# Transposes of the probabilities two bursts behind their scores, values one burst later, in a hybrid decoder trunk

## The chip, the cores and the metric

The kernel runs on one core of a Trainium2 chip. The metric is device time in microseconds (us) of one execution, the median of several runs.

## What is computed

The reference is a two-layer decoder trunk for one sequence of 1024 positions and width 1024, in fp32. Layer 0 feeds one projection into a dilated attention with 16 heads of 64 and a pooling branch, each gated, and projects back; layer 1 does the same with a spatial gating unit and an S5 state-space layer. After each comes a cross-attention into 256 memory tokens. The change touches the dilated attention alone:

```python
sc = jnp.einsum('nbihd,nbjhd->nbhij', qb, kb, preferred_element_type=jnp.float32)
sc = jnp.where(valid[None, :, None], sc, NEG)
m = jnp.max(sc, axis=-1, keepdims=True)
p = jnp.exp(sc - m)
den = jnp.sum(p, axis=-1, keepdims=True)
o = jnp.einsum('nbhij,nbjhd->nbihd', (p / den).astype(v.dtype), vb)
...
a_out = dilated_attention(q, k, v).reshape(b, s, A_WIDTH) * jax.nn.silu(g_a)
```

The three patterns (windows 128, 512, 2048 with dilations 1, 4, 16) are mixed by their softmax denominators.

## The kernel before

Large products are made of three matmuls each (high x high, high x low, low x high part of an fp32 number), with a moving tile of 128x512; a projection half (one 512-wide half of the sequence for one block of 128 channels) is 8 such triples, 24 matmuls, `mm3` at lines 206 to 208, or lines 472 to 474 for the values' own projection. Weights come by SP's queue, ScalarE makes the high part (line 180), VectorE the low part (line 181).

In the first layer's stage two generators run interleaved. `ab_main` is the projections, gates and the pooling branch. `ab_side` is the attention: 8 pairs of heads with 8 blocks of 128 queries each, so 64 bursts, numbered `n`; a burst does both heads of a pair (called halves here). `drive` takes one step of the side for about every two steps of the main, so TensorE's order has in most gaps between bursts 24 projection matmuls, in about one of six 12. The order of TensorE within the stage is then pinned as recorded (`in_order`); on the other engines a scheduler decides it.

A burst's work is in four functions made by `attn`:

- `front(b)`: the scores, 32 small matmuls into two PSUM buffers `ps_s` (line 536); VectorE adds the mask into an SBUF tile `P` and so reads the buffers (line 543), joins the two dilated parts (546), takes the maximum (547); ScalarE exponentiates (548), VectorE inverts the sum (549), ScalarE scales (550).
- `turn(b)`: per half, TensorE transposes `P` into a PSUM buffer `ps_t` (lines 567 and 570); VectorE copies the near part to `PT` (576), ScalarE the far part to `PTr` (580), which GpSimd has zeroed (563).
- `mix(b)`, every second burst: the values for two bursts, `PT` against `V`, into `ps_o` (line 593).
- `last(half)`, every fourth burst: the far values (line 605), then VectorE multiplies by the gate (609) and `put_g` stores the result from GpSimd's queue (621).

The tags `ps_mm`, `ps_s`, `ps_t` and `ps_o` have two PSUM buffers each. `P`, `PT`, the gated results and other half-size tiles share 14 SBUF buffers. GpSimd meanwhile prepares tables for the S5 layer (`s5_prep`, started from `behind`); it uses two of the same PSUM tags, with transposes at line 1154, copied by ScalarE at line 1155.

In the loop of `ab_side` before, step `n` issues the transposes of burst `n - 1`, then the scores of burst `n`, and on odd steps the values of bursts `n - 3` and `n - 2`.

Of the kernel before, what the change touches and what calls it, by code (L numbers as in the profile page):

```python
# [98 lines left out]
class Prog:  # L99
# [524 lines left out]
    def ab_side(s):  # L624


        prep, made = s.s5_prep(), {}
        for n in range(64 + 2):
            pr, b = divmod(n, 8)
            if n < 64:  # L630
                while pr not in s.pair or (b == 3 and pr not in s.gated):
                    yield 0
                if b == 0:
                    made[pr] = s.attn(pr)
            if 0 < n <= 64:
                was, wb = divmod(n - 1, 8)
                made[was][1](wb)
            if n < 64:
                made[pr][0](b)
            if n > 2 and n % 2 == 1:  # L640
                was, wb = divmod(n - 3, 8)
                made[was][2](wb)
                if n % 4 == 1:
                    made[was][3](wb // 4)
            yield 1
            if n > 6 and n < 64:
                s.behind(prep)
        while s.behind(prep) is not None:
            yield 1
# [912 lines left out]
```

## Time and profile before

| | us |
|---|---|
| median of 3 runs | 2097.26 |
| lowest, highest | 2096.18, 2103.48 |
| the profiled execution | 2095.89 |
| its span, first to last instruction | 2094.0 |

The profile is of one execution. Busy times are per engine; PE is TensorE's matmuls, PEld its weight loads, DVE is VectorE, ACT ScalarE, POOL GpSimd, and DVEq is VectorE's sequencer. Matmuls overlap in the pipeline, so the distance of their starts is the measure of their pace, not their length. An idle time in brackets stands before the instruction, with what ended it.

### The profile page before, as it was taken

To read this page: it belongs to the slowest core of one execution; us is meant where nothing else is said; L and a number is where in the kernel's file an instruction comes from. 1 tells how busy PE (TensorE), PEld (TensorE's weight loads), DVE (VectorE), ACT (ScalarE), POOL (GpSimd) and SP (SyncE) were. 2 spreads that over 40 slices of the span, in tenths; PEclk is the share of its full clock that TensorE was granted. 3 is DMA by queue.
4 is the path that set the end of the run, shared out by engine and by line. 5 is a ranking of instruction groups with operands and counts; after the bars stand their busy time and mean duration, and the time that the engine had idled before them with its cause. 6 is when DMAs were issued, how large, how long until landed. Compare 5 with 4: busy or idle time off the path is not lost. (4 is left out here: it accounts for less than half of the span.)

```text
span 2094.0 us, 31894 instructions
## 1 busy us (share of the span) xinstructions
PE 2035.1 (97%) x12350; PEld 1686.6 (81%) x12350; DVE 1094.8 (52%) x1987; ACT 803.3 (38%) x1618; POOL 532.7 (25%) x802
## 2 busy tenths in 40 slices
PE   8999999999999988999999999999999999999998
PEld 8998877777776766888888888888888887888887
DVE  6665055645456565456444555444653335554544
ACT  7766134355334443114333443212221123434443
POOL 5332006822334255221111003221221100210013
PEclk9999999999999989999999999999999999999999
DMA  8888202113122122116444035522431125641142
GB/s 300 302 284 293 86 30 64 62 56 117 53 78 74 56 77 86 69 73 240 163 165 166 31 126 181 175 91 71 137 98 68 66 95 172 206 156 70 56 166 81
DMA packets 129159, 258.68 MB, mean 124 GB/s; under 512 B 12784, under 2 KB 58992, under 8 KB 129008
## 3 DMA queue, kind: packets, MB, share of 16 engines
q1 hardware_dynamic: 86608, 189.52, 26.7%
q0 software_dynamic: 13440, 43.53, 5.6%
q10 hardware_dynamic: 28960, 23.60, 3.6%
q8 instruction: 97, 1.59, 0.3%
q14 instruction: 54, 0.44, 0.1%
HBM read 193.16 MB, written 63.44 MB: 123 GB/s over the span
## 5 line engine op out<-in xcount | busy, mean ns | idle before, releaser
L181 DVE TENSOR_TENSOR wl<-wst,wh 128x1024 fp32r<-128x1024 f32 (+1 forms) x263 | 348.6, 1339 | 112.7 <-ACT wh L180 108.3
L206 PE MATMUL ps_mm<-xg,wh 128*128 128x512 f32 x928 | 371.8, 401 | 1.9 <-DVE ug L1367 1.5
L207 PE MATMUL ps_mm<-xg,wh 128*128 128x512 f32 x928 | 364.7, 393 | 0.0
L208 PE MATMUL ps_mm<-xg,wl 128*128 128x512 f32 x928 | 364.2, 392 | 0.0
L180 ACT ACTIVATE wh<-wst 128x1024 fp32r<-128x1024 f32 (+1 forms) x263 | 262.6, 1016 | 103.0 <-PE ps_mm L207 82.7
L206 PEld LDWEIGHTS ps_mm<-xg,wh 128*128 128x128 f32 x928 | 175.7, 189 | 47.8 <-issue 8.5
L208 PEld LDWEIGHTS ps_mm<-xg,wl 128*128 128x128 f32 x928 | 175.7, 189 | 37.1
L207 PEld LDWEIGHTS ps_mm<-xg,wh 128*128 128x128 f32 x928 | 175.9, 190 | 34.6 <-issue 0.2
L243 POOL TENSOR_TENSOR acc<-acc,sq 128x512 f32<-128x512 f32 (+1 forms) x81 | 103.6, 1279 | 212.5 <-ACT sq L239 206.2
L226 ACT ACTIVATE xg<-x,gains 128x512 fp32r<-128x512 f32 x64 | 46.2, 722 | 240.0 <-DVE x L782 182.9
L548 ACT ACTIVATE P<-P,mx 128x192 f32<-128x192 f32 (+7 forms) x128 | 65.8, 515 | 137.4 <-DVE mx L547 136.1
L580 ACT ACTIVATE PTr<-ps_t 128x128 f32<-128x128 f32 (+2 forms) x192 | 43.1, 271 | 159.2 <-DVE PT L576 154.8
L576 DVE TENSOR_TENSOR PT<-ps_t,cst 128x256 f32<-128x256 f32 (+1 forms) x128 | 47.0, 402 | 61.5 <-PE ps_t L570 61.1
L543 DVE TENSOR_TENSOR P<-ps_s,cst 128x320 f32<-128x320 f32 (+7 forms) x128 | 65.3, 551 | 19.0 <-PE ps_s L536 17.6
L227 DVE SCALAR_TENSOR_TENSOR xg<-x,gains,xg 128x512 fp32r<-128x512 f32 x64 | 52.4, 819 | 43.1 <-ACT xg L226 43.1
L621 POOL DMA_DIRECT2D gab<-G x32 | 18.4, 574 | 207.9 <-DVE G L609 83.6
L1367 DVE TENSOR_TENSOR ug<-ps_mm,R 128x512 f32<-128x512 f32 x32 | 22.1, 689 | 90.4 <-PE ps_mm L208 90.3
L567 PE MATMUL ps_t<-cst,P 128*128 128x128 f32 x128 | 36.0, 293 | 33.6 <-ACT P L550 30.8
L207 PE MATMUL ps_s<-gr,wh 128*128 128x512 f32 x168 | 65.6, 390 | 2.0 <-DVE gr L214 2.0
L206 PE MATMUL ps_s<-gr,wh 128*128 128x512 f32 x168 | 65.5, 390 | 1.2 <-ACT gr L213 1.2
L208 PE MATMUL ps_s<-gr,wl 128*128 128x512 f32 x168 | 65.4, 389 | 0.0
L550 ACT ACTIVATE P<-P,den 128x192 f32<-128x192 f32 (+7 forms) x128 | 60.3, 510 | 10.0 <-DVE den L549 10.0
(424 smaller groups left out, 4878.0 us busy)
## 6 DMA issues: line engine op xcount, KB each, us to landing
wst<-w_ab SPq DMA_DIRECT2D x40, 512.0 KB, 3.3
wst<-w_out_ab SPq DMA_DIRECT2D x32, 512.0 KB, 3.8
wst<-vsc SPq DMA_DIRECT2D x32, 512.0 KB, 4.0
wst<-w_kv SPq DMA_DIRECT2D x31, 512.0 KB, 6.3
wst<-w_cd SPq DMA_DIRECT2D x24, 512.0 KB, 3.7
wst<-w_out_cd SPq DMA_DIRECT2D x32, 384.0 KB, 3.6
wst<-w_q SPq DMA_DIRECT2D x16, 512.0 KB, 8.3
msc<-mo ACTq DMA_DIRECT2D x32, 256.0 KB, 6.3
```

Of the source, the lines that this page charges most:

```text
L180: s.last_hi = s.nc.scalar.activation(H[:, :w], t[:, :w], AF.Copy)
L181: s.nc.vector.tensor_tensor(L[:, :w], t[:, :w], H[:, :w], op=ALU.subtract)
L206: s.nc.tensor.matmul(ps, lhsT=lh, rhs=rh, start=(i == 0), stop=False)
L207: s.nc.tensor.matmul(ps, lhsT=lh, rhs=rl, start=False, stop=False)
L208: s.nc.tensor.matmul(ps, lhsT=ll, rhs=rh, start=False, stop=(i == n - 1))
L226: nc.scalar.activation(H, x, AF.Copy, scale=g)
L227: nc.vector.scalar_tensor_tensor(L, x, g, H, op0=ALU.mult, op1=ALU.subtract)
L243: nc.gpsimd.tensor_tensor(st["acc"][:, :n], st["acc"][:, :n], q[:, :n], op=ALU.add)
L543: nc.vector.tensor_tensor(t[:, :n], p[e][:, :n], s.cst[:, m0:m0 + n], op=ALU.add)
L548: j = nc.scalar.activation(t[:, :m], t[:, :m], AF.Exp, bias=mx, accum_out=den)
L550: k = nc.scalar.activation(t[:, :m], t[:, :m], AF.Copy, scale=den)
L576: nc.vector.tensor_tensor(PT[b // 2, e][:, c0 + 128 * j0:c0 + 256].rearrange("p (j i) -> p j i", i=128), src, s.cst[:, C_NM + 128 * j0:C_N ...
```

## The change

The side's loop issues the transposes of burst `n - 2` at step `n` instead of `n - 1`. The values follow on even steps instead of odd ones, one step later, and the loop is one step longer.

```diff
-        for n in range(64 + 2):
+        for n in range(64 + 3):
...
-            if 0 < n <= 64:
-                was, wb = divmod(n - 1, 8)
+            if 1 < n <= 65:
+                was, wb = divmod(n - 2, 8)
                 made[was][1](wb)
             if n < 64:
                 made[pr][0](b)
-            if n > 2 and n % 2 == 1:
-                was, wb = divmod(n - 3, 8)
+            if n > 3 and n % 2 == 0:
+                was, wb = divmod(n - 4, 8)
                 made[was][2](wb)
-                if n % 4 == 1:
+                if n % 4 == 2:
                     made[was][3](wb // 4)
```

TensorE's order at the start of attention, where the second burst's scores stand (a piece of the difference; `ps_t<-cst,P` is a transpose of probabilities, `ps_s<-kk,q` scores, `ps_mm` a projection):

```order
 L207 MATMUL ps_mm<-xg_1548,wh 128x512
 L208 MATMUL ps_mm<-xg_1548,wl 128x512
-L567 MATMUL ps_t<-cst,P 128x128
-L570 MATMUL ps_t<-cst,P 128x128
-L567 MATMUL ps_t<-cst,P 128x128
-L570 MATMUL ps_t<-cst,P 128x128
 L536 MATMUL ps_s<-kk,q 32x256 x8
 L536 MATMUL ps_s<-kk,q 32x64 x8
```

The first burst's transposes have left the place ahead of the second burst's scores; they stand ahead of the third burst's now, and each later burst's likewise.

VectorE's order around the sixteenth burst's first pass (line 543, width 512), with buffer numbers; `PT<-ps_t` copies a transpose. Before:

```order
330 L543 TENSOR_TENSOR P_4354<-ps_s_4336,cst_84 128x512
331 L543 TENSOR_TENSOR P_4363<-ps_s_4337,cst_84 128x512
332 L181 TENSOR_TENSOR wl_4463<-wst_4292,wh_4462 128x1024
333 L546 TENSOR_TENSOR P_4354<-P_4354 128x128
334 L546 TENSOR_TENSOR P_4363<-P_4363 128x128
335 L547 TENSOR_REDUCE mx_4355<-P_4354 128x1
336 L547 TENSOR_REDUCE mx_4364<-P_4363 128x1
337 L549 RECIPROCAL den_4356<-den_4356 128x1
338 L549 RECIPROCAL den_4365<-den_4365 128x1
339 L576 TENSOR_TENSOR PT_4324<-ps_t_4401,cst_84 128x256
```

And now:

```order
328 L543 TENSOR_TENSOR P_4338<-ps_s_4320,cst_84 128x512
329 L543 TENSOR_TENSOR P_4347<-ps_s_4321,cst_84 128x512
330 L181 TENSOR_TENSOR wl_4449<-wst_4278,wh_4448 128x1024
331 L546 TENSOR_TENSOR P_4338<-P_4338 128x128
332 L546 TENSOR_TENSOR P_4347<-P_4347 128x128
333 L547 TENSOR_REDUCE mx_4339<-P_4338 128x1
334 L576 TENSOR_TENSOR PT_4382<-ps_t_4378,cst_84 128x256
335 L576 TENSOR_TENSOR PT_4390<-ps_t_4386,cst_84 128x256
336 L547 TENSOR_REDUCE mx_4348<-P_4347 128x1
337 L549 RECIPROCAL den_4340<-den_4340 128x1
338 L543 TENSOR_TENSOR P_4412<-ps_s_4394,cst_84 128x160
```

The copies of the previous burst's transposes now stand between the two halves' maxima (line 547); before, both maxima and both reciprocals came ahead of the next copies.

TensorE's order after the last scores of the attention; `ps_o<-PT,V` are values. Before:

```order
L536 MATMUL ps_s<-kk,q 32x256 x16
L593 MATMUL ps_o<-PT,V 64x128 x2
L593 MATMUL ps_o<-PT,V 64x256 x2
L593 MATMUL ps_o<-PT,V 64x128 x2
L206 MATMUL ps_mm<-plr,wh 128x512
L207 MATMUL ps_mm<-plr,wh 128x512
```

And now:

```order
L208 MATMUL ps_mm<-plr,wl 128x512
L567 MATMUL ps_t<-cst,P 128x128
L570 MATMUL ps_t<-cst,P 128x128 x2
L567 MATMUL ps_t<-cst,P 128x128
L570 MATMUL ps_t<-cst,P 128x128 x2
L593 MATMUL ps_o<-PT,V 64x128 x2
L593 MATMUL ps_o<-PT,V 64x256 x2
L593 MATMUL ps_o<-PT,V 64x128 x2
```

The values that stood right behind the last scores now stand behind the transposes that follow six projection matmuls later.

## Rows read from the trace of the kernel before

**Rows 1.** The page's first part: busy us, share of the span, instructions.

```profile
PE 2035.1 (97%) x12350; PEld 1686.6 (81%) x12350; DVE 1094.8 (52%) x1987; ACT 803.3 (38%) x1618; POOL 532.7 (25%) x802
```

**Rows 2.** Stretches: length, then PE, PEld, DVE, ACT, POOL busy; clock, DMA share, GB/s.

```profile
270.00:825.00 555.00, 520.57 (x4680) 401.86 (x4679) 318.44 (x771) 242.56 (x655) 232.22 (x477) 0.96 0.21 68
...
570.00:590.00 20.00, 15.54 (x125) 11.16 (x131) 11.79 (x27) 8.62 (x23) 1.15 (x2) 0.83 0.30 91
...
740.00:750.00 10.00, 8.91 (x66) 7.09 (x66) 3.36 (x13) 3.61 (x12) 10.00 (x36) 0.83 0.01 2
760.00:780.00 20.00, 13.06 (x109) 9.20 (x110) 14.39 (x28) 9.71 (x27) 9.32 (x15) 0.74 0.41 146
800.00:820.00 20.00, 14.75 (x92) 10.01 (x90) 9.15 (x21) 7.09 (x21) 12.32 (x17) 0.83 0.33 119
```

**Rows 3.** Waits of TensorE, 270 to 825 us: total us, times, longest.

```profile
PE ps_t L567 <- ACT P L550: 30.8, 15, 4.1
PE ps_t L567 <- ACT s5wz L1155: 2.7, 1, 2.7
```

**Rows 4.** Timeline of TensorE, a quiet burst: start, us, instruction.

```profile
443.66 1.04 PE L536 MATMUL ps_s<-kk,q 64*32 64x256 f32 x32
...
450.22 0.27 PE L567 MATMUL ps_t<-cst,P 128*128 128x128 f32 x1
```

**Rows 5.** Timeline of TensorE, scores and transposes at waits, idle in brackets.

```profile
424.26 0.93 PE L536 MATMUL ps_s<-kk,q 64*32 64x256 f32 x32
...
431.91 0.47 PE L567 MATMUL ps_t<-cst,P 128*128 128x128 f32 x1 [3.79 <-ACT P L550]
...
433.06 0.47 PE L567 MATMUL ps_t<-cst,P 128*128 128x128 f32 x1 [0.24 <-ACT P L550]
...
575.88 0.48 PE L567 MATMUL ps_t<-cst,P 128*128 128x128 f32 x1 [2.66 <-ACT P L550]
...
577.74 0.48 PE L567 MATMUL ps_t<-cst,P 128*128 128x128 f32 x1 [0.95 <-ACT P L550]
...
750.18 0.77 PE L536 MATMUL ps_s<-kk,q 64*32 64x256 f32 x32
...
762.88 0.45 PE L567 MATMUL ps_t<-cst,P 128*128 128x128 f32 x1 [3.50 <-ACT P L550]
...
767.60 0.48 PE L567 MATMUL ps_t<-cst,P 128*128 128x128 f32 x1 [4.06 <-ACT P L550]
...
804.97 0.48 PE L567 MATMUL ps_t<-cst,P 128*128 128x128 f32 x1 [3.69 <-ACT P L550]
```

**Rows 6.** Timeline of TensorE, projection matmuls after the wait at 767.

```profile
771.02 0.63 PE L206 MATMUL ps_mm<-xg,wh 128*128 128x512 f32 x1
...
772.30 0.63 PE L206 MATMUL ps_mm<-xg,wh 128*128 128x512 f32 x1
```

**Rows 7.** Timelines of VectorE and GpSimd, 750 to 768 us.

```profile
750.86 6.31 DVE L708 TENSOR_TENSOR win<-vb 128x1023 f32<-128x1023 f32 x1
...
762.08 4.91 DVE L181 TENSOR_TENSOR wl<-wst,wh 128x512 fp32r<-128x512 f32 x1 [1.17 <-ACT wh L180]
...
754.04 2.04 POOL L938 TENSOR_TENSOR s5w<-Ei,trig 128x512 f32<-128x512 f32 x2
...
765.18 1.25 POOL L938 TENSOR_TENSOR Ei<-s5w,s5w 128x512 f32<-128x512 f32 x1
```

**Rows 8.** Timelines of TensorE, VectorE, ScalarE: one burst's scores to its probabilities.

```profile
475.45 0.83 PE L536 MATMUL ps_s<-kk,q 64*32 64x256 f32 x32
...
476.37 0.96 DVE L543 TENSOR_TENSOR P<-ps_s,cst 128x352 f32<-128x352 f32 x2 [0.27 <-PE ps_s L536]
...
479.00 0.84 ACT L550 ACTIVATE P<-P,den 128x224 f32<-128x224 f32 x2
```

**Rows 9.** Line 543: waits in VectorE's queue, ns min/median/max.

```profile
L543 DVEq EVENT_SEMAPHORE  x35: 21/21/1022, 271.5 to 783.4; - x35
```

**Rows 10.** DMA issues of the gates' stores: count, KB each, us to landing.

```profile
gab<-G POOLq DMA_DIRECT2D x32, 256.0 KB, 2.5
```

## The prediction

> **What bounds the kernel now.** I read the busy shares first: TensorE is busy 97% of the span, VectorE 52%, ScalarE 38%, GpSimd 25% [rows 1]. So only what TensorE waits for, or does slowly, can be won. The table of stretches puts the loss in one place: the attention stage, 270 to 825 us, is the long stretch with a lowered granted clock, 0.96, and 34 us without a matmul (555.0 less 520.6) [rows 2]. The list of who waited for whom, for TensorE in that stretch, names it: 30.8 us in 15 waits of the probabilities' first transpose (line 567) for ScalarE's last pass over the same probabilities (line 550), then 2.7 us in one wait of that transpose for the S5 preparation's copy (line 1155), and next to nothing else [rows 3].
>
> The timeline of TensorE shows the pattern. In a quiet burst the scores (line 536) end at 444.70 and the transposes of that burst start at 450.22, with 24 projection matmuls between: 5.5 us, 0.23 us each, and no wait [rows 4]. The probabilities are ready some 3.6 us after the scores (scores end 476.28, line 550 ends 479.84) when VectorE and ScalarE are free [rows 8], so 5.5 us suffices. About every sixth gap holds 12 matmuls, 2.8 us, and in some places the two engines are late as well; there TensorE stands. Five waits make 17.7 of the 30.8 us [rows 5]. After most of them the projection matmuls start 0.427 us apart instead of 0.23 (three in 1.28 us) [rows 6], and the 10 or 20 us around show a granted clock of 0.74 to 0.83 [rows 2]: a wait is paid twice, once standing and once at the 1.2 GHz level of the two.
>
> **The change part by part.** No instruction is added or removed. *Transposes two bursts behind.* The first burst's transposes now follow the scores of two further bursts, as the first piece of TensorE's order shows; from then on each burst's transposes are separated from its scores by one more gap, one more set of scores and transposes. That adds at least 2.8 + 0.4 + 0.5 = 3.7 us, mostly 6.5. At 424 to 432 us the scores ended at 425.19 and the transposes began at 431.91, 6.7 us later [rows 5]. The new distance there is 2.8 us (12 matmuls), the next transposes and scores of about 1.6, and 24 matmuls of 5.5, so 9.9 us: covered. The same sum covers the waits at 575.88 (a 12-matmul gap too) and 804.97, the latter with little to spare. So I take the 30.8 us as removed, before what is given back.
>
> *The clock.* The deficits are 4 x 1.7 (10 us at 0.83, of which the row from 740 stands for four, the others from 300, 430 and 670), 3.4 (570 to 590), 5.2 (760 to 780) and 3.4 (800 to 820), 18.8 us [rows 2]. A stretch at half clock costs half its length, which is this deficit, only where TensorE was working. In three of the windows it stood for 4.06, 0.95 and 0.24 us between slow transposes [rows 5], which takes half of those off, 2.6 us. So 16.2 us go with the waits, if all go. Together 47.0 us.
>
> *What stays.* At 750.95 the scores end, and the two halves of their probabilities come at 762.9 and 767.6 [rows 5]. The new distance is 24 matmuls 5.5, transposes and scores 1.4, values and far values 2.9, 12 matmuls 2.8: 12.6 us, so 763.5. The first half is in time, the second 4 us late. Its cause is no queue distance: a VectorE add took 6.31 us and a split of weights 4.91 us, and each ended about a microsecond after a row of GpSimd's work did (757.2 after 756.1, 767.0 after 766.4) [rows 7]; that work is not touched. I leave the 4.06 us and the slow stretch behind it (twice 5.2 us at half clock, less the standing, halved: 3.2 us) in the sum: 7.3 us. The S5 wait of 2.7 us is not the change's and stays.
>
> *Values one burst later.* They moved with the transposes: in the order's last piece the values follow the transposes of a later burst, and between a transpose and the values that use it lies one gap, as before. VectorE's copy and ScalarE's copies have that gap still. At the end of attention the last far values come after 24 more projection matmuls; more of these follow, so nothing stands. The gates' stores on GpSimd's queue follow a step later, and are read only in the output projection. Cost nought; with the cover gone it would be one gap, 5.5 us, once.
>
> *New waits.* The transposes had held the next scores back until the previous probabilities were done. Now the scores wait only for VectorE to have read their two PSUM buffers (line 543). It does so 1.05 us after the scores when free [rows 8] against a gap of at least 2.8, so nought is the lower end; where a VectorE instruction is held up as at 750 us it is up to 6.3 less 2.8, 3.5 us in a place [rows 7]. Nearer the first: 2 us in all, an estimate.
>
> Sum: 30.8 + 16.2 - 7.3 - 2 = 37.7 us. The profiled execution took 2095.9 us (span 2094.0), 1.4 under the median of the runs shown; from its own time, 2058 us.
>
> **The rivals.** *The other engines become the late ones.* VectorE's new order at the second place shows the second half's maximum of a burst standing behind the copies of the previous burst's transposes, which TensorE issues only before the next scores; so probabilities come later there by most of a gap, and part of the new distance is spent. If this and the GpSimd collisions keep the three worst places (4.06 + 3.50, 3.69, 2.66 + 0.95 us standing; 3.2 + 3.4 + 2.9 slow), 24.4 us stay and the gain is 22.6: 2073 us. For it: these three have VectorE or ScalarE late, not only a short gap. Against: in the order the displaced maxima still come a gap ahead of their own transposes. The Trainium skill ("SBUF — State Buffer", the section on the two separate sides) says that VectorE and GpSimd share a port pair under an exclusive lock, so the loser stands for the whole of the other's instruction. The 6.31 us add agrees in kind, and spans several GpSimd rows in sequence [rows 7]; by this rule collisions move but do not vanish.
>
> *The buffers run out, and it is slower.* A probability tile lives a burst longer, so two more of the 14 half-size buffers are taken, and VectorE's first pass (line 543) may stand until a gate's store on GpSimd's queue has freed one. Up to a delay of about 5.5 - 1.05 = 4.5 us the gap hides it; beyond that the scores stand. GpSimd works through the preparation for 10 us and more without a break (10.00 of 10 from 740) [rows 2], and a gate's store lands 2.5 us after its issue [rows 10]: 10 + 2.5 - 4.5 = 8 us lost per case, so from six such cases on (48 against 47 us) the change is slower; at twelve, of the 16 gates stored in the stage, 2096 - 47 + 96 = 2145 us. Against: before, VectorE's queue stood at most 1.02 us for anything ahead of that pass [rows 9], and as many of these instructions wait for such a store in the new order (17) as in the old. The Trainium skill ("Perfetto Trace Analysis", Optimization Strategy) reads a gap that repeats on the saturated engine as a possible lack of SBUF or PSUM for the next tile. By that the waits would not be cured by distance and could grow. Here the waits name line 550's data, not a buffer [rows 3].
>
> *The waits change their name only.* If VectorE and ScalarE could not keep up on average, TensorE would stand at the scores for the same sum: 2096 us. They are busy 57% and 44% of the stage (318.4 and 242.6 of 555.0) [rows 2], so this is unlikely.
>
> **How the numbers follow.** The forecast, 2058 us, has 0.60, the late engines 0.27, the renamed wait 0.08, the buffers 0.05. The lower end of the range is all 47.0 us and the S5 wait of 2.7 with 1.7 of slow clock, 51.4: 2044 us. The upper takes in the late engines with room for half as much again of what stays, 24.4 x 1.4 = 34, a gain of 13: 2083 us. Outside lie the last two cases and a tail of the second. Half a percent, 10.5 us, is about what a measurement of this kernel can tell from no change. Faster by more: all of the first and nearly all of the second, 0.86; within: 0.09; slower: 0.05.
>
> **What would show it.** Right, if the list of TensorE's waits between 270 and 825 us has under 8 us left for line 567 behind line 550, the granted clock of the stage is 0.98 or more, and the stage ends 35 to 40 us earlier while the rest of the span keeps its length. The wait that stays would stand where the pooling's first adds meet GpSimd's rows. The second case shows as waits of line 567 that remain at three or four places, with VectorE rows of 2 to 6 us ahead of them. The third shows as waits of line 536 behind line 543 and of VectorE behind GpSimd or a store. The forecast is wrong if the waits go and the time doesn't, which would mean that a later stage waits for something that attention used to be slower than.

## The result and the profile after

The changed kernel takes 2059.99 us (2057.86 to 2062.47, four runs), against 2098.97 us (2096.18 to 2103.48) of the kernel before: ratio 0.9823, 95% interval 0.9807 to 0.984. The forecast was 2058, the range 2044 to 2083. The profiled executions have spans of 2094.0 and 2057.4 us, so 36.6 us are to be accounted for. One of the four executions of the run called e4 below took 7101 us and is left out; its time is the median of the other three.

The page of the kernel after: busy us, share of the span and instructions.

```profile
PE 2020.7 (98%) x12350; PEld 1680.1 (82%) x12350; DVE 1102.9 (54%) x1987; ACT 800.2 (39%) x1618; POOL 539.9 (26%) x802
```

The same instructions run [rows 1]; TensorE's busy time is 14.4 us shorter with as many matmuls, the first sign of a faster clock. The stretches of the kernel after, attention's stage and two lowered pieces of it: length, then PE, PEld, DVE, ACT, POOL busy; clock, DMA share, GB/s.

```profile
270.00:785.00 515.00, 503.09 (x4632) 392.26 (x4631) 325.55 (x768) 238.38 (x651) 234.63 (x472) 0.99 0.22 70
...
490.00:500.00 10.00, 7.39 (x76) 5.75 (x77) 5.73 (x14) 5.24 (x16) 0.61 (x1) 0.83 0.28 83
690.00:700.00 10.00, 9.12 (x70) 6.72 (x69) 7.43 (x22) 4.00 (x10) 4.34 (x5) 0.83 0.03 8
```

TensorE stands 11.9 us in the stage (515.0 less 503.1) instead of 34.4 [rows 2], and those two are the only 10 us pieces with a lowered clock; in all others of the stage it is 1.00. What TensorE still waits for, from the list of who waited for whom in the stage of the kernel after (us in total, times, longest):

```profile
PE ps_t L567 <- ACT s5wz L1155: 5.1, 2, 3.5
PE ps_t L1154 <- ACT PTr L580: 2.6, 2, 2.4
PE ps_t L567 <- ACT PTr L580: 1.8, 3, 1.2
PE ps_mm L206 <- DVE G L738: 1.4, 1, 1.4
PE ps_s L536 <- DVE ktr L1165: 0.9, 1, 0.9
```

The line that led this list before, line 567 behind line 550 [rows 3], is gone. All five rows are new or longer, and three of them are about the two buffers `ps_t`, not about the probabilities (the row of `s5wz` had 2.7 us [rows 3], that of line 1154 0.8).

The gain is kept to the end. Line 842 is a matmul of the cross-attention behind the first layer; its group, with the first and last start, in the kernel before:

```profile
L842 PE MATMUL ps_o<-wh,xg x96: 387/389/481, 1140.8 to 1989.2; 128*128 128x512 f32 x96
```

and in the kernel after:

```profile
L842 PE MATMUL ps_o<-wh,xg x96: 387/389/481, 1105.6 to 1952.9; 128*128 128x512 f32 x96
```

Its first one starts 35.2 us earlier and its last 36.3 us, so the rest of the program keeps its length to about a microsecond.

### The profile page after: what moved, and what is told of

It reads as the page before. It is cut to its first block, busy times and chain, and to the rows that moved or that the text cites. A ratio compares the mean times of both kernels' runs of the same rounds, so it can differ in the third digit from the quotient of the medians.

```text
span 2057.4 us, 31828 instructions
## 1 busy us (share of the span) xinstructions
PE 2020.7 (98%) x12350; PEld 1680.1 (82%) x12350; DVE 1102.9 (54%) x1987; ACT 800.2 (39%) x1618; POOL 539.9 (26%) x802
## 4 chain that ended last, share of the span: by engine, by line
PE 86%; DVE 5%; ACT 2%; issue 1%; DMA 1%; POOL 1%; DVEq 0%; ACTq 0%; POOLq 0%
PE ps_mm L206 13%; PE ps_mm L207 13%; PE ps_mm L208 13%; PE ps_s L207 4%; PE ps_s L208 4%; PE ps_s L206 4%; PE ps_o L208 3%; PE ps_o L207 3%; PE ps_o L206 3%; PE ps_s L536 2%; PE ps_mm L1340 1%; PE ps_mm L1338 1%; PE ps_mm L1339 1%; PE ps_o L593 1%; PE ps_mm L472 1%
## 5 line engine op out<-in xcount | busy, mean ns | idle before, releaser
L208 PEld LDWEIGHTS ps_mm<-xg,wl 128*128 128x128 f32 x928 | 174.3, 188 | 36.9
L1367 DVE TENSOR_TENSOR ug<-ps_mm,R 128x512 f32<-128x512 f32 x32 | 22.1, 689 | 90.4 <-PE ps_mm L208 90.3
L239 ACT ACTIVATE sq<-x 128x512 f32<-128x512 f32 (+1 forms) x77 | 44.8, 582 | 42.6 <-DVE x L890 37.9
L536 PE MATMUL ps_s<-kk,q 64*32 64x256 f32 (+7 forms) x2048 | 58.4, 332 | 0.9 <-DVE ktr L1165 0.9
```

The source lines that it names most:

```text
L208: s.nc.tensor.matmul(ps, lhsT=ll, rhs=rh, start=False, stop=(i == n - 1))
L536: i = nc.tensor.matmul(p[e][32 * r:32 * r + 32, c], lhsT=q[rows[e], 128 * b + 32 * r:128 * b + 32 * r + 32], rhs=x, start=True, stop=True)
```

## A ledger of the runs

Two sums tell nearly every span below. *Standing* is TensorE's idle time from 270 to 830 us. *Slow* is the sum, over the 56 pieces of 10 us there, of 10 us times one less the granted clock. Where a piece was both idle and slow a little is counted twice (2.6 us before).

| kernel | standing | slow | sum | span |
|---|---|---|---|---|
| before | 34.4 | 20.4 | 54.8 | 2094.0 |
| e1, even gaps, one behind | 29.1 | 10.2 | 39.3 | 2078.8 |
| e12, values later alone | 45.0 | 25.3 | 70.3 | 2107.2 |
| e2, values left on odd steps | 22.1 | 13.7 | 35.8 | 2075.8 |
| e3, change in the second half | 19.4 | 8.5 | 27.9 | 2071.9 |
| after | 11.9 | 3.4 | 15.3 | 2057.4 |
| e4, S5 transposes in the projections' PSUM | 8.5 | 3.4 | 11.9 | 2055.3 |
| e6, 16 half-size and 41 large buffers | 8.8 | 3.4 | 12.2 | 2057.5 |
| e5, three behind, buffers of e6 | 16.6 | 5.1 | 21.7 | 2070.0 |
| e7, 13 half-size buffers | 26.5 | 11.9 | 38.4 | 2084.4 |
| e9, two half-size buffers freed | 6.4 | 0.0 | 6.4 | 2047.9 |
| e11, e9 with even gaps | 10.5 | 5.1 | 15.6 | 2057.5 |
| e10, before, with the buffers of e9 | 39.8 | 22.1 | 61.9 | 2099.2 |

Span less sum lies between 2037 and 2048 us throughout, though the spans differ by 59. One run is not in the table: e8, without the S5 preparation in the stage, loses its time behind 830 us. Between before and after, 22.5 us of standing and 17.0 of slow clock make 39.5; less the 2.6 that were counted twice, 36.9 of the 36.6 us.

## Is it the short gaps, or the distance?

The theory was that a burst's probabilities come too late over a gap of 12 matmuls, so that a distance of two bursts, or simply no short gap, would cure it. The first run keeps the order of before and makes all gaps but two 24 matmuls long.

```diff
-        drive(tc, s.ab_main(), s.ab_side(), 0.55, -500)
+        drive(tc, s.ab_main(), s.ab_side(), 0.5, -500)
```

> The kernel before, transposes one burst behind, but with a side rate of 0.5 instead of 0.55, so that all gaps between bursts but two near the end hold 24 projection matmuls. Theory (the waits came from gaps of 12 matmuls that are shorter than the probabilities' latency): the waits at gaps of 12 were 2.20 + 2.03 + 4.03 + 0.30 + 3.61 + 2.03 + 3.69 + 1.56 = 19.5 us of the 30.8, with 11 us of slow clock behind them; most of that goes, so 25 to 30 us faster than before, about 2070, and 10 us behind the change. Rival (VectorE and ScalarE are late whatever the gap): under 10 us faster, 2090.

Measured: 2080.8 us, ratio 0.993 (0.9903 to 0.9956). TensorE's waits in the stage of this kernel:

```profile
PE ps_t L567 <- ACT P L550: 28.7, 13, 9.0
PE ps_t L567 <- ACT s5wz L1155: 0.4, 1, 0.4
```

The two waits of the last burst, from its timeline of TensorE:

```profile
812.27 0.47 PE L567 MATMUL ps_t<-cst,P 128*128 128x128 f32 x1 [8.96 <-ACT P L550]
...
815.82 0.48 PE L567 MATMUL ps_t<-cst,P 128*128 128x128 f32 x1 [2.64 <-ACT P L550]
```

The standing behind line 550 hardly shrank, 28.7 us against 30.8 [rows 3]; the slow clock halved. Of the 28.7 us, 11.6 are these two, where in this order the pooling's add stands beside GpSimd's preparation and takes 3.73 us (at 796.26). The rest is spread: nine of the eleven longest waits are between 0.95 and 2.64 us. The gain of 15.7 us lies between what the theory and the rival gave. So the short gaps were under half of the story: one burst behind, even 24 matmuls are too short wherever VectorE or ScalarE is late. The distance itself was needed.

The next run makes the change from burst 32 on only.

```diff
-            if 1 < n <= 65:
-                was, wb = divmod(n - 2, 8)
-                made[was][1](wb)
+            for t in (n - 1, n - 2):
+                if 0 <= t < 64 and t + (1 if t < 32 else 2) == n:
+                    made[t // 8][1](t % 8)
...
-            if n > 3 and n % 2 == 0:
-                was, wb = divmod(n - 4, 8)
-                made[was][2](wb)
-                if n % 4 == 2:
-                    made[was][3](wb // 4)
+            for t in (n - 3, n - 4):
+                if 0 <= t < 64 and t % 2 == 0 and t + (3 if t < 32 else 4) == n:
+                    made[t // 8][2](t % 8)
+                    if t % 4 == 2:
+                        made[t // 8][3](t % 8 // 4)
```

> The change for bursts 32 to 63 only; bursts 0 to 31 keep their transposes one behind. Theory (each wait is local, so gains add up by place): the waits of bursts 0 to 31, 9.9 us in the trace of before, and the slow clock behind two of them, 3.3 us, come back: 13 us more than the change, 2073. Rival (what counts is the later part, where VectorE meets GpSimd's preparation): 2062.

Measured: 2073.2 us, ratio 0.9888 (0.9862 to 0.9915). The first row of its waits:

```profile
PE ps_t L567 <- ACT P L550: 9.7, 7, 3.8
```

The waits are local: behind line 550, those of the half that keeps the old distance stay, the others go, and the time follows.

## Do the values have to move along?

The prediction put the values' move at no cost and took it as part of the whole. Two runs part them. First the change with the values left on odd steps:

```diff
-        for n in range(64 + 3):
+        for n in range(64 + 2):
...
-            if n > 3 and n % 2 == 0:
-                was, wb = divmod(n - 4, 8)
+            if n > 2 and n % 2 == 1:
+                was, wb = divmod(n - 3, 8)
...
-                if n % 4 == 2:
+                if n % 4 == 1:
```

> Transposes two bursts behind as in the change, values left on their odd steps, so that they use transposes made only one set of scores (about 1 us) earlier. Theory (the values' step had to move along because VectorE's and ScalarE's copies need 1 to 2 us after the transposes): values wait 0.3 us in 32 places and far values 0.3 in 16, some 15 us, 2068 to 2075, with waits of lines 593 and 605 behind lines 576 and 580. Rival (that part of the change does nothing): 2060, as the change.

Measured: 2077.59 us, ratio 0.9913 (0.9888 to 0.9937). Its waits begin with

```profile
PE ps_o L593 <- DVE PT L576: 9.1, 8, 5.5
PE ps_t L567 <- ACT PTr L580: 6.9, 1, 6.9
PE ps_t L567 <- ACT s5wz L1155: 2.9, 1, 2.9
```

The values now follow the transposes of their own burst with one set of scores between, and TensorE waits for VectorE's copy of the transpose (line 576). The kernel loses 17.6 us of the gain, much as expected, but not in the way expected, by 0.3 us in every place. Line 593 waits in eight places: six times 0.2 to 0.5 us, once 1.80 and once 5.47, the last where VectorE's join (line 546) takes 4.96 us at 784.00. And the 6.9 us of the second row stand behind a pooling's add that in this order is longer than in any other run here, from its timeline of VectorE:

```profile
730.74 9.56 DVE L708 TENSOR_TENSOR win<-vb 128x1023 f32<-128x1023 f32 x1
```

So the values' place is shown to cost the 9.1 us of the first row and the slow clock behind them; how much of the rest comes from where the collision fell, this run does not tell.

Then the other half alone: transposes one burst behind as before, values one step later.

```diff
-        for n in range(64 + 2):
+        for n in range(64 + 3):
...
-            if n > 2 and n % 2 == 1:
-                was, wb = divmod(n - 3, 8)
+            if n > 3 and n % 2 == 0:
+                was, wb = divmod(n - 4, 8)
...
-                if n % 4 == 1:
+                if n % 4 == 2:
```

> The kernel before with only the values one step later, transposes still one behind. Theory (values never waited, so moving them alone does nothing): 2097, within 4. Rival (their later place opens a gap that helps the transposes): 2085 to 2092.

Measured: 2109.29 us, ratio 1.0051 (1.0033 to 1.0069): slower, and a miss. The largest two waits, from its timeline of TensorE:

```profile
769.32 0.48 PE L567 MATMUL ps_t<-cst,P 128*128 128x128 f32 x1 [7.44 <-ACT P L550]
...
816.69 0.47 PE L567 MATMUL ps_t<-cst,P 128*128 128x128 f32 x1 [5.25 <-ACT P L550]
```

All its waits are of line 567 behind line 550, 41.6 us between 265 and 825 us. The values of two bursts, 1 to 3 us of TensorE's work, stand between a burst's scores and its transposes and so are part of the distance. Before they stood behind odd-numbered bursts, counted from 0; here behind even ones. Compared burst by burst, the waits behind bursts 9, 15, 29, 35, 47, 55 and 61 grew by 1.4 to 3.0 us each, those behind 4, 20 and 36 fell by 0.8 to 2.3. Two bursts don't fit. Burst 43 is odd, and its wait for the S5 copy fell by 2.1. Burst 62, whose wait is the second row, has values behind it now and its wait still grew, from 3.69 [rows 5]; there VectorE's two joins (line 546) took 6.6 us beside GpSimd's preparation, where they took 1.7 before. So the moved cover explains most of the loss, and why it is missed more behind odd bursts than it helps behind even ones stays open.

So neither half is worth the whole: the values alone cost some 11 us, the transposes alone bring 19, both together 39.

## What are the new waits?

The list of after names ScalarE's copies out of `ps_t`. The largest, from the timeline of TensorE in the kernel after:

```profile
485.38 0.63 PE L1154 MATMUL ps_t<-cst,s5W 128*128 128x128 f32 x4 [0.21 <-ACT PTr L580]
...
488.61 0.27 PE L567 MATMUL ps_t<-cst,P 128*128 128x128 f32 x1
...
492.61 0.33 PE L567 MATMUL ps_t<-cst,P 128*128 128x128 f32 x1 [3.52 <-ACT s5wz L1155]
...
563.28 0.63 PE L1154 MATMUL ps_t<-cst,s5W 128*128 128x128 f32 x4 [2.39 <-ACT PTr L580]
...
692.14 1.86 PE L1160 MATMUL ps_s<-s5o,s5W 128*128 128x16 f32 x16
...
695.42 1.74 PE L536 MATMUL ps_s<-kk,q 64*32 64x256 f32 x30 [0.88 <-DVE ktr L1165]
...
743.05 0.33 PE L567 MATMUL ps_t<-cst,P 128*128 128x128 f32 x1 [1.17 <-ACT PTr L580]
```

The S5 preparation's transpose filled one `ps_t` at 485.4; the burst's first half took the other at 488.6; the second half stands until ScalarE has copied the S5 transpose out. The timeline of ScalarE there shows why that is late:

```profile
490.99 0.55 ACT L548 ACTIVATE P<-P,mx 128x320 f32<-128x320 f32 x1
...
491.54 0.54 ACT L550 ACTIVATE P<-P,den 128x320 f32<-128x320 f32 x1
491.99 0.57 ACT L1155 ACTIVATE s5wz<-ps_t 128x512 f32<-128x512 f32 x1
```

The copy (line 1155) stands in ScalarE's order behind the exponential of a later burst's second half. And that is late in part because of VectorE:

```profile
485.18 0.61 DVE L543 TENSOR_TENSOR P<-ps_s,cst 128x448 f32<-128x448 f32 x1
...
487.30 0.62 DVE L543 TENSOR_TENSOR P<-ps_s,cst 128x448 f32<-128x448 f32 x1 [1.18 <-DMA v<-vt]
...
489.68 0.49 DVE L547 TENSOR_REDUCE mx<-P 128x1 f32<-128x320 f32 x1
```

The second half's `P` had no buffer: line 543 waited for a store of projected values, `v<-vt`, to free one. The view of line 543 in the kernel after sums what VectorE waited for ahead of it (us, times):

```profile
  PE ps_s L536: 9.7, 18
  DMA s5k<-ktr: 3.7, 1
  PE ps_o L593: 2.6, 3
  DMA v<-vt: 2.5, 3
  DMA gab<-G: 2.1, 1
```

The last four rows, 10.9 us, are waits for a buffer; before, the same view had none of them. The next runs ask which resource it is. First the S5 transposes in the projections' PSUM buffers:

```diff
-                p = s.ps("t")
+                p = s.ps("mm")
```

> The change, with the S5 preparation's transposes (line 1154) put into the projections' PSUM tag instead of the one that the probabilities' transposes use. Theory (what is left of TensorE's waits after the change, 5.1 + 2.6 us and most of the slow clock left, comes from sharing two PSUM buffers with the preparation): these waits go, 6 to 9 us less, 2052. Rival (the wait only moves to the projections, which then lack a buffer): 2060 or up to 5 more.

Measured: 2057.58 us, ratio 0.9814 (0.979 to 0.9839), which its interval does not tell from the change (0.9823). Its waits begin:

```profile
PE ps_mm L1154 <- ACT vt L482: 2.9, 1, 2.9
PE ps_t L567 <- ACT PTr L580: 1.8, 2, 1.5
PE ps_mm L1154 <- DVE P L543: 1.5, 1, 1.5
```

The 7.7 us of the S5 preparation's two rows became 4.4 us at the other tag. PSUM is mostly where the lateness shows, not where it comes from. Then the half-size SBUF buffers, one fewer:

```diff
-NU = 14
+NU = 13
```

> The change with 13 half-size buffers instead of 14. Theory (they do not bind): 2060, within 4. Rival (14 is just enough, and a late store of a gated result holds up VectorE's first pass): 10 us or more slower, 2070 to 2085, with waits of line 536 behind line 543.

Measured: 2079.19 us, ratio 0.9918 (0.989 to 0.9947), 19 us above the change. Its waits begin:

```profile
PE ps_t L567 <- ACT s5wz L1155: 14.0, 3, 6.5
PE ps_t L567 <- ACT PTr L580: 5.2, 5, 2.2
PE ps_s L536 <- DVE ktr L1165: 2.5, 2, 1.4
PE ps_s L536 <- DVE P L543: 2.3, 3, 1.1
```

The same rows, grown: one buffer takes the first from 5.1 to 14.0 us, in an execution of 2086.11 us, the longest of the four; the others took 2078 to 2080. The rival had the size right, and the place wrong: line 536 stands behind line 543 for 2.3 us only. And two more, paid for with one of the 42 large ones:

```diff
-NB = 42
-NU = 14
+NB = 41
+NU = 16
```

> The change with 16 half-size and 41 full-size buffers: the control for three bursts behind. Theory (half-size buffers do not bind in the change): 2060, within 4. Rival (the longer life of the probabilities makes VectorE wait for buffers, some of which reaches TensorE): 2050 to 2055.

Measured: 2060.49 us, ratio 0.9823 (0.9794 to 0.9853), the change's own time, but not because the buffers do not bind. The waits of `s5wz` are gone and line 842 first starts at 1099.0 instead of 1105.6. That lead of 6.6 us is lost again later, nearly half of it at one place, from the list of TensorE's waits behind 800 us:

```profile
PE ps_mm L206 <- DVE ug L1367: 4.1, 1, 4.1
```

The kernel after has 1.0 us in this row, and so has e9 below, which keeps the 42 large buffers. That points at the missing large one; no run shows the tile. To free two without taking any, the factor 0.125 on the queries, which lived in two half-size tiles, was put into the split of their weights:

```diff
+        key = s.plan[i][0]
+        if key[0] == "ab" and key[1] < 8:
+            s.last_hi = s.nc.scalar.activation(H[:, :w], t[:, :w], AF.Copy, scale=0.125)
+            s.nc.vector.scalar_tensor_tensor(L[:, :w], t[:, :w], 0.125, H[:, :w], op0=ALU.mult, op1=ALU.subtract)
...
-        held, R8 = {}, s.R8
+        held = {}
...
-                                               R8[h].rearrange("p (b i r) -> p b r i", b=4, r=4), op=ALU.mult)
+                                               s.R[h].rearrange("p (b i r) -> p b r i", b=4, r=4), op=ALU.mult)
...
-        s.R8 = [s.u("R8") for _ in range(2)]
-        for h in range(2):
-            s.nc.gpsimd.tensor_scalar(s.R8[h], s.R[h], 0.125, None, op0=ALU.mult)
```

> The change with two half-size buffers freed, 42 full-size ones kept: the scale of 0.125 on the queries is put into the split of their weights, so its two tiles of 128x512 are not held through the stage. Theory (the waits left of transposes for the S5 copy come from a late buffer, by way of ScalarE's order, and the 16-buffer control lost its 6.7 us again only because it has one full-size buffer less): attention's last far values at 786 as in that control, the rest as in the change, 2053. Rival (the gain in the stage is always given back later): 2060.

Measured: 2050.77 us (2048.92 to 2052.03), ratio 0.9775 (0.976 to 0.9791). The edit shifts line numbers by two to five: 572 is 567, 585 is 580, 1156 is 1154. Its waits in the stage:

```profile
PE ps_t L572 <- ACT PTr L585: 1.8, 3, 1.2
PE ps_t L1156 <- ACT PTr L585: 1.8, 1, 1.8
PE ps_mm L211 <- DVE G L740: 1.4, 1, 1.4
```

No `s5wz` is left and no piece of the stage has a lowered clock. The view of VectorE's first pass (548 is 543) has one row of waiting left, that for the scores:

```profile
  PE ps_s L541: 10.1, 20
```

So VectorE's waits for a buffer are gone, and TensorE's for the S5 copy with them. The scheduler's order is another one too: at the largest wait of the kernel after a split of weights (line 180) stands between the two exponentials and a scaling ahead of the copy; here the copy, at 485.41, follows the two exponentials at once. What of the lateness was the missing buffer itself and what the order set around it, the runs do not part. It beats both kernels, by 9 us the changed one. The same edit on the kernel before tells whether this is the buffers or the edit:

> The kernel before, with the same two buffers freed. Theory (one burst behind, buffers are not what TensorE waits for): within 5 us of the kernel before, 2097. Rival (part of the waits before was for buffers too): 2085 to 2090.

Measured: 2096.19 us, ratio 0.9995 (0.9977 to 1.0012): nothing. One burst behind, 14 half-size buffers are enough; two behind, 14 are just short.

## Further, and without the neighbour

Three bursts behind, with the buffers of e6, which is therefore its control:

```diff
-        for n in range(64 + 3):
+        for n in range(64 + 4):
...
-            if 1 < n <= 65:
-                was, wb = divmod(n - 2, 8)
+            if 2 < n <= 66:
+                was, wb = divmod(n - 3, 8)
...
-            if n > 3 and n % 2 == 0:
-                was, wb = divmod(n - 4, 8)
+            if n > 4 and n % 2 == 1:
+                was, wb = divmod(n - 5, 8)
...
-                if n % 4 == 2:
+                if n % 4 == 3:
```

> Transposes three bursts behind their scores, values again one later; since the probabilities live longer, 16 half-size and 41 full-size buffers instead of 14 and 42 (with 14 this order cannot run). Theory (two bursts already cover the probabilities' latency; what is left of TensorE's waits is for PSUM shared with the S5 preparation): as the control with the same buffers, within 5 us, 2060. Rival (TensorE would still profit from distance, since late probabilities only just come in time): 5 to 10 us faster than the control.

Measured: 2072.19 us, ratio 0.9875 (0.9849 to 0.9901), 12 us slower than e6, a miss for both theories. There was no wait behind line 550 left to remove, and each further burst behind holds two more buffers: of its waits `s5wz` is back with 4.1 us, and line 567 behind `PTr` has 7.8 (4.9 in e6). VectorE's waits for a buffer at line 543 are back too, 8.6 us against none in e6. A part is the collision once more: the pooling's add took 9.25 us, and 2.31 us of standing at 738.77 and 1.73 at 744.70 come behind it.

With the S5 preparation issued behind the attention instead of beside it:

```diff
-            if n > 6 and n < 64:
-                s.behind(prep)
```

> The change without the S5 preparation in the attention stage: all of it is issued after attention. Theory (TensorE's remaining waits in that stage are the preparation's: 5.1 + 2.6 + 0.9 us and 3.4 us of slow clock; and VectorE's rows of 2 to 4 us come from GpSimd's work): the last far values, at 793 us, end near 781, and the long VectorE rows are gone from the stage. The whole kernel may be anything from 2045 to 2100, since the preparation then lies in a later stage. Rival (the waits are those of crowded VectorE and ScalarE queues): the stage as long as before, 793 give or take 3.

Measured: 2145.8 us, ratio 1.0229 (1.0204 to 1.0254). A stretch of its attention:

```profile
275.00:765.00 490.00, 490.00 (x4566) 383.90 (x4566) 291.56 (x739) 234.56 (x647) 30.41 (x54) 1.00 0.20 61
```

TensorE never stands there and its clock never falls; attention's last far values start at 766.6 instead of 793.0 us. So the waits that the change left come with the preparation, all but one: the wait for the pooling's gate (`G`, 1.4 us in the list of after) is there again at 804.55, with 2.1 us. Whether they come by VectorE's collisions with GpSimd, by the shared PSUM tag or by the half-size tile that the preparation takes, this run does not part. The 26 us are twice what was expected: besides the stage's standing and slow clock, 15.3 us in the ledger, the preparation's own matmuls have left (lines 1154 and 1160, 12.4 us busy in the stage of after). That work has to be done somewhere. Done later, it has less to hide behind; the longest of its own waits, behind 800 us:

```profile
PE ps_t L1152 <- POOL s5W L936: 44.6, 4, 15.0
```

That row alone takes back more than the 26 us.

Last, e9 with even gaps (the edit of e1):

> The change with two buffers freed and a side rate of 0.5, so that all gaps but a few hold 24 projection matmuls. Theory (at two bursts behind the distance is ample, so the gaps' evenness brings nothing more): as with two buffers freed alone, within 5 us, 2053. Rival (gaps of 12 still cost, through the PSUM of the transposes): 5 to 8 less, 2046.

Measured: 2057.82 us, ratio 0.9808 (0.9787 to 0.9828): 7 us slower than e9, a miss for both theories. Two waits at the end of its attention, in the timeline of TensorE, make 5.7 us:

```profile
792.77 0.33 PE L572 MATMUL ps_t<-cst,P 128*128 128x128 f32 x1 [2.97 <-ACT PTr L585]
...
796.00 0.48 PE L572 MATMUL ps_t<-cst,P 128*128 128x128 f32 x1 [2.69 <-ACT P L555]
```

and the timeline of VectorE shows the pooling's add and the probabilities' join beside GpSimd's preparation, as in [rows 7]:

```profile
776.42 3.68 DVE L710 TENSOR_TENSOR win<-vb 128x1023 f32<-128x1023 f32 x1
...
784.55 2.18 DVE L551 TENSOR_TENSOR P<-P 128x128 f32<-128x128 f32 x2
```

With even gaps the attention ends 25 us later, and the collision falls on its last burst, whose transposes have no later scores in front of them. The clock falls too: 5.1 us of slow against none in e9, 3.4 of them from 790 to 810 us.

## Why the prediction was right, point by point

- *The 30.8 us of waits go.* Right: line 567 waits for line 550 no longer, and e1 and e3 show that it is the distance, place by place. The working by gaps of 12 and 24 matmuls was too kind to 24: e1, with hardly a gap of 12, still stood 28.7 us.
- *The slow clock goes with them, 16.2 us.* Right in kind and nearly in size: after the 3.2 left at the collision, 13.0 were forecast; the lowered pieces fell from 20.4 to 3.4 us, 14.4 without the part counted twice. Among them is a piece at 640 us, worth 1.7 us and behind the S5 wait, that the prediction had let stand. The remaining 3.4 stand behind other waits than forecast.
- *What stays, 7.3 us at the pooling's add.* Mis-sized. The add was 4.12 us long this time, and its largest trace on TensorE is the 1.17 us at 743.05: VectorE's maxima came late, and the copies of the previous transposes (line 580, at 742.73) stood behind the exponential in ScalarE's order. The collision itself is real; e11 shows it again where no distance covers it.
- *New waits, 2 us.* Mis-sized the other way, and named wrongly. The scores did wait little (0.9 us). But the S5 preparation's and the bursts' transposes share `ps_t`, and the prediction never followed ScalarE's order there. All standing was to be 9.6 us (4.06 + 2.7 + 2 + the 0.8 of line 1154 behind line 580, left aside) and was 11.8. The collision was put 6 us too high (7.3 against 1.2), the other waits 8.5 us too low (10.6 standing and 3.4 slow against 2 + 2.7 + 0.8); the errors cancel, so that the total is better than its parts, and that is luck.
- *The values' move costs nothing.* Right for the whole change, but not because the move is idle: without it 17.6 us are lost (e2, in part by the collision), and by itself it costs 11 (e12).
- *The buffers run out.* Given 0.05, and it is the larger part of what still limits the changed kernel. The place and price were wrong: not twelve blocked scores of 8 us, but, at the largest wait, a `P` late by a microsecond, a copy queued behind it, and a transpose that wants the copied buffer. The decisive point lies one buffer away, not at six such cases: one fewer costs 19 us more, two freed give 9 back. The Trainium skill ("Perfetto Trace Analysis", Optimization Strategy) reads a repeating gap as a possible lack of memory for the next tile. For the kernel before the runs speak against it (e10, 0.9995); for the kernel after it holds (e9).
- *The late engines* (0.27) and *the renamed wait* (0.08) did not come: no wait behind line 550 or at the scores of that size.

What would show it came as written: no wait of that pair, a stage clock of 0.99, the next stage 35.2 us earlier, the rest unchanged. One sign of the buffers came beside it, at a price too small to upset the sum: VectorE's waits for stores at line 543, 8.3 us (3.7 + 2.5 + 2.1).

## What to carry to other kernels

When the saturated engine waits for a chain on other engines, put a second unit of work between producer and consumer, and move the consumer's own consumer by as much. Then count the buffers that the longer life takes: the lack shows not where the tile is made but at a neighbour that shares an engine's queue or a PSUM tag. Test it from both sides, one buffer fewer and two more.

## What was not expected of the hardware

- In these runs the length of a wait alone does not tell whether the clock falls after it. In the kernel after, 2.39 us at 563.28 was followed by no lowered piece, 0.88 us at 695.42 by one of 0.83 (690 to 700); in e1, 2.27 us at 621 by none. What ran ahead differs: the 0.88 us came behind sixteen matmuls of width 16 (line 1160, at 692.14) and the first scores. Why the one fell and the others did not stays open.
- ScalarE's switch between the gates' function and the exponential took 1.28 us each way, and TensorE's wait of 2.39 us, which ends at 563.28, stands behind the first of them, the gate's 1.06 us and the copy. From the timeline of ScalarE in the kernel after:

```profile
560.62 1.28 ACT L555 ACT_TABLE_LOAD   x1
...
563.31 1.28 ACT L548 ACT_TABLE_LOAD   x1
```
